# A tuned two-layer matrix kernel: the last third of w1 loaded as float32 by SyncE's queue and cast on chip, x's second half loaded after four strips of w1, five sums of x on GpSimd

## The chip, the cores and the metric

The kernel runs on one core of a Trainium2 chip. The metric is the device time of one execution in microseconds. Before the change three runs gave 852.94, 865.14 and 854.82 us, a median of 854.82 us. The engines are called as in the profile: PE is TensorE (matmuls), PEld its weight loads, DVE VectorE, ACT ScalarE, POOL GpSimd, SP SyncE, which computes nothing and issues transfers. A "q" behind an engine's name is the part of it that issues and waits.

## The reference

x has 16 x 512 = 8192 rows of 768 numbers, w1 is 768 x 3072, w2 is 3072 x 768, all float32.

```python
y = np.matmul(x, w1) + b1
y = np.maximum(y, 0)
return np.matmul(y, w2).astype(np.float32)
```

## The kernel before, in words

Both layers run in float16 with float32 sums in PSUM. Each layer is cut into blocks and multiplied with a bilinear scheme that needs 26 block products where the plain way needs 32. The price is sums: for one block of x 19 sums of blocks (`X_SUMS`, `next_x_sums`, L787, the instruction at L799), for one third of w1 18 sums (`W1_SUMS`, `add_w1_sums`, L807, instruction L811), for one third of w2 18 (`add_w2_part`, L854, instruction L876), and sums of the products on the way out of PSUM.

**First layer.** x is worked in 8 blocks of 1024 rows. w1 has 3072 columns, in three thirds (g = 0, 1, 2) of four strips of 256 columns: strips 0 to 3 are g = 0, 4 to 7 are g = 1, 8 to 11 are g = 2. A strip is 768 x 256 numbers, loaded by one transfer (`load_strip`, L693) from GpSimd's queue, which casts to float16 on the way. It fills two slots of the tile `v`. For blocks 1 to 7 each third is 26 products of six matmuls of 256 columns (L1127), whose results leave PSUM by ACT (L1150, L1155) and DVE (L1161, L1164) into `yo`, 12 slots that lie in the tile `z`. From there they are stored to a scratch tensor `yd` in DRAM by SP's or GpSimd's queue (`add_store_y`, L998, issue L1003).

**Block 0** is special, since w1 is still arriving. Its thirds 0 and 1 are computed the plain way, strip by strip (`plain`, L1011, matmuls L1022, out through ACT at L1036): a unit is one half of a strip's columns times one half of the block's rows, six matmuls of 512 columns or twelve of 256. Third 2 uses the 26 products. The first half of the block's rows (x tiles 0 to 3) comes as float32 over SP's and ACT's queues, the second half (tiles 4 to 7) as two casting transfers over GpSimd's queue (`load_x`, L710, issue L712). Both are transposed on PE (L948). `first_block` (L1058) writes the order of block 0 by hand: EARLY strips with the first half of the rows, the transposes of the second half, these strips with the second half, then the other strips of thirds 0 and 1 with both.

**Blocks 1 to 7** get x row by row: a casting load of 128 rows by GpSimd's queue (`add_load_x`, L765), then a transposing transfer by SP's queue (`add_turn`, L770, issue L774), which must follow the load; `add_rows` is both. Then come the 19 sums.

**Second layer.** 16 half blocks, each 26 products of six matmuls of 384 columns (L1322), with y read back from `yd` by SP's queue and summed by DVE (L1280).

**What sets the order.** The program is a list of tasks with their reads and writes. `Graph.run` (L375) is a planner: it lays the tasks of each engine in an order by assumed durations and assumed landing times (`presets`, L740, holds those of the prologue's loads), and `emit` writes the instructions out in that order. On the chip each engine works through its list strictly in order, and each transfer takes one of eight semaphores of its queue in turn, so an engine that issues a transfer first waits until the transfer eight before it on that queue has landed. `plan` (L1464) says what is put among the products of which block: for block b the loads and transposes of block b + 1 stand in `later` and are added in `between` (L1207). A constant such as `W2_POOL` lists which sums of w2 GpSimd does instead of DVE.

Of the kernel before, what the change touches and what calls it, by code (L numbers as in the profile page):

```python
# [18 lines left out]
P = 128  # L19
# [559 lines left out]
EARLY, AHEAD = 5, 8  # L579

POOL_X = ()
# [6 lines left out]
W2_POOL = ((0, 11), (0, 13), (0, 18), (0, 23), (0, 25), (1, 13), (1, 25))  # L588
# [5 lines left out]
X1_LATE = 2.0  # L594
# [13 lines left out]
class Fast:  # L608
# [93 lines left out]

    def add_stage_w2(self, g, q, h):
        h0 = (6 * q + 2 * g + h) * P
        self.g.add("POOL", 850, lambda: self.nc.gpsimd.dma_start(
            out=self.w2dram[:, g, q:q + 5:4, h * self.NH:(h + 1) * self.NH],
            in_=self.w2[h0:h0 + P, :].rearrange("p (a n) -> p a n", a=2)), lat=15.0, dma=1.4,
            writes=[("w2d", g, q, h)], after=[self.g.last_pe])
# [11 lines left out]
    def prologue(self):  # L720
        nc = self.nc
        for s in range(4):
            (nc.sync, nc.scalar)[s % 2].dma_start(out=self.rows(s),
                                                  in_=self.xf[s * P:(s + 1) * P, :])
            if s == 1:
                self.load_bias()
        self.constants()
        self.load_strip(0, 0, 2)
        self.load_strip(0, 1, 2)
        for strip in range(2, EARLY):  # L730
            self.load_strip(*divmod(strip, 4))
        for s in (4, 6):
            self.load_x(0, s, NZ - 8 + s, 2)
        for strip in range(EARLY, 12):
            self.load_strip(*divmod(strip, 4))
        for _ in range(9):
            nc.tensor.matmul(self.ps[:, 7, 0:P], lhsT=self.ones, rhs=self.ones, start=True,
                             stop=True)

    def presets(self):  # L740
        g = self.g
        at = (9.5, 11.5, 13.5, 15.5, 19.3, 27.6, 30.6, 32.5, 35.8, 39.1, 41.9, 44.8)
        for t in range(12):
            for k in range(2):
                g.preset(("v", t // 4, 2 * (t % 4) + k), at[t] - (0 if t > 1 or k else 1.0))
        for s in range(4):
            for h in range(2):
                g.preset(("z", NZ - 4 + s, h), 21.9 if s < 2 else 24.6)
# [38 lines left out]
    def next_x_sums(self, b, limit=99):  # L787

        slot = self.xs[b]
        while self.todo and self.free and limit:  # L790
# [5 lines left out]
            e = "POOL" if n in POOL_X else "DVE"  # L796
# [5 lines left out]
            self.g.add(e, 552 if e == "DVE" else 2000, add, port=True,  # L802
# [51 lines left out]
    def add_w2_part(self, g):  # L854
# [15 lines left out]
        for groups in FUSE_V2[g]:  # L870
            for o, i, j, sign in left:
# [7 lines left out]
                self.g.add(e, 2400 if e == "POOL" else 151 + 400 * len(groups), add, port=True,  # L879
# [178 lines left out]
    def first_block(self):  # L1058
# [20 lines left out]
        for strip in range(2):  # L1079
# [3 lines left out]
            run(*pair)  # L1083
        early = [plain(strip, j, 0, 2 if strip == 2 else 1)
# [7 lines left out]
        for p in late[1:]:  # L1092
            next(p)
        run(*late, plain(1, 1, 1, 2),
            *(plain(strip, j, 1, 2 if strip == 2 else 1)
              for strip in range(2, EARLY) for j in range(2)))
        self.xs[0] = self.raw_slots(0)
        self.rowed1 = 8 * (self.rowed + list(self.scratch.values()))
        rest = [(strip, m, j) for strip in range(EARLY, 4 * PLAIN) for m in range(2)
                for j in range(2)]  # L1100
        loads = list(range(8 if PLAIN > 1 else 0))
        for strip, m, j in rest:
            if loads:
                self.add_rows(1, loads.pop(0))
            run(plain(strip, j, m))
        for s in loads:
            self.add_rows(1, s)
# [356 lines left out]
    def plan(self):  # L1464
# [10 lines left out]
        for b in range(NB):  # L1475
# [4 lines left out]
            elif b + 1 < NB:  # L1480
                assert not self.todo
                pre = PRE if b > 1 else 0
# [5 lines left out]
                if b + 2 < NB and b:  # L1488
                    self.later += [(2, PRE_AT + PRE_GAP * s, self.add_load_x, (b + 2, s))
                                   for s in range(PRE)]  # L1490
                for n in range(STAGES if b else 0):
                    if staged:
                        self.later.append((*divmod(STAGE_AT + (78 - STAGE_AT) * n // STAGES, 26),
                                           self.add_stage_w2, staged.pop(0)))
            for n in range(EARLY_RATE if b > 2 else 0):
# [94 lines left out]
```

## Time and profile before

| what | before |
|---|---|
| median of 3 runs | 854.82 us (852.94 to 865.14) |
| the profiled execution | 857.22 us, of which 855.6 us is the span from the first to the last instruction |
| PE busy | 837.6 us, 98% of the span |
| DVE, ACT, POOL busy | 701.8, 558.6, 237.7 us |
| granted TensorE clock | 0.999 |
| queue of SP (q1), share of 16 DMA engines | 120.26 MB, 47.0% |
| queue of POOL (q0), share of 16 DMA engines | 71.00 MB, 43.8% |

The page divides the span by engine, by slices of time and by groups of instructions. A row of a group has the line, the engine, the operation, what it writes from what, how many of them, then busy time, mean duration in ns, and the idle time of the engine just before them with what ended it. A row of the timeline has start, duration, engine, line and operation, and in brackets the idle time before it with the releaser. A row of the table by windows has start and end, the length, then for each engine the busy time and the number of instructions, the granted clock, the busy share of the DMA engines (above 1 where packets of several queues overlap) and GB/s. MB counts what is written, so a casting load reads twice that.

### The profile page before, as it was taken

The page shows a single profiled execution, that of the slowest core. Times are in us where ns is not written, and L with a number is a line of the kernel's source. Part 1 is how long each engine was busy: PE and PEld are TensorE (multiplying, and loading weights), DVE is VectorE, ACT ScalarE, POOL GpSimd, SP SyncE. Part 2 cuts the span into 40 slices and gives each one's busy share as a digit, 9 for nine tenths or more (in the row PEclk, how much of TensorE's full clock was granted, in tenths as well). Part 3 has the DMA queues.
Part 4 walks back from the last instruction along what each step waited for, and adds up shares of the span by engine and source line. Part 5 has one row for each costly group of instructions (what it writes and reads, how often), then busy time and mean ns, then how long its engine had stood idle before and what let it go on. Part 6 is the DMA issues. An engine that isn't in the chain of part 4 may idle for free. (4 is left out here: it accounts for less than half of the span.)

```text
span 855.6 us, 17854 instructions
## 1 busy us (share of the span) xinstructions
PE 837.6 (98%) x6263; PEld 612.6 (72%) x6263; DVE 701.8 (82%) x1341; ACT 558.6 (65%) x1252; POOL 237.7 (28%) x400
## 2 busy tenths in 40 slices
PE   8999989999999999999999999999999999999998
PEld 7658878888888888888875666566666665565664
DVE  6869779797988989889899988888777788777773
ACT  4557767878787878787873455565645567757421
POOL 6104455544645446442402201011100011101000
PEclk9999999999999999999999999999999999999999
DMA  9997999999999999998888989978889989988622
GB/s 218 228 229 166 173 229 229 209 217 228 221 216 225 217 221 234 221 282 271 264 254 202 263 271 281 258 207 230 230 244 277 267 209 222 253 219 274 227 74 75
DMA packets 169168, 193.32 MB, mean 226 GB/s; under 512 B 58556, under 2 KB 144644, under 8 KB 169076
## 3 DMA queue, kind: packets, MB, share of 16 engines
q1 hardware_dynamic: 113632, 120.26, 47.0%
q0 software_dynamic: 54976, 71.00, 43.8%
q8 instruction: 49, 0.80, 0.4%
q10 hardware_dynamic: 468, 0.90, 0.3%
q14 instruction: 43, 0.35, 0.1%
HBM read 140.39 MB, written 83.95 MB: 262 GB/s over the span
## 5 line engine op out<-in xcount | busy, mean ns | idle before, releaser
L1322 PE MATMUL ps<-v,z 128*128 128x384 f16 x2496 | 407.1, 326 | 1.7 <-DVE ps L1343 1.0
L1127 PE MATMUL ps<-z,v 128*128 128x256 f16 x3432 | 379.9, 273 | 8.1 <-DVE z L1161 3.1
L1127 PEld LDWEIGHTS <-v 128*128 128x128 f16 x3432 | 335.0, 98 | 53.3 <-issue 10.8
L1322 PEld LDWEIGHTS <-z 128*128 128x128 f16 x2496 | 244.0, 98 | 164.0 <-issue 1.8
L1280 DVE TENSOR_TENSOR z<-z 128x768 f16<-128x768 f16 x448 | 232.7, 553 | 41.7 <-PE ps L1322 23.5
L1003 POOL DMA_DIRECT2D yd<-z x228 | 123.6, 545 | 173.6 <-ACT z L1150 72.1
L1161 DVE CUSTOM_DVE_ANT_0 z<-ps,s 128x512 f16<-128x512 f32 x220 | 143.8, 684 | 25.8 <-PE ps L1127 21.4
L1155 ACT ACTIVATE s<-ps,bt 128x256 f32<-128x256 f32 x352 | 146.6, 478 | 16.2 <-PE ps L1127 10.6
L1339 ACT ACTIVATE s<-ps 128x384 f32<-128x384 f32 (+1 forms) x151 | 73.6, 488 | 121.4 <-PE ps L1322 114.4
L1164 DVE TENSOR_TENSOR s<-ps,s 128x512 f32<-128x512 f32 x132 | 88.8, 683 | 4.6 <-PE ps L1127 3.3
L799 DVE TENSOR_TENSOR z<-z 128x768 f16<-128x768 f16 x152 | 78.2, 551 | 7.5 <-PE ps L1127 6.7
L908 ACT ACTIVATE junk<-z 128x768 f16<-128x768 f16 x94 | 78.8, 838 | 0.9
L1339 ACT ACTIVATE ps<-ps 128x384 f32<-128x384 f32 x80 | 38.0, 475 | 62.5 <-PE ps L1322 59.6
L904 POOL DMA_DIRECT2D z<-in_x_dram x32 | 23.3, 751 | 193.3 <-ACT junk L908 188.1
L1343 DVE TENSOR_TENSOR s<-ps,s 128x384 f32<-128x384 f32 x107 | 59.3, 554 | 13.2 <-PE ps L1322 12.9
L1155 ACT ACTIVATE z<-ps,bt 128x256 f16<-128x256 f32 x132 | 55.3, 497 | 9.8 <-DVE s L1164 9.8
L1164 DVE TENSOR_TENSOR ps<-ps,s 128x512 f32<-128x512 f32 x66 | 45.2, 697 | 16.6 <-ACT s L1155 13.2
L1155 ACT ACTIVATE ps<-ps,bt 128x256 f32<-128x256 f32 x88 | 39.5, 448 | 25.5 <-PE ps L1127 20.6
L1150 ACT ACTIVATE s<-ps 128x512 f32<-128x512 f32 x66 | 39.7, 602 | 21.5 <-DVE z L1161 14.8
L1343 DVE TENSOR_TENSOR s<-s,ps 128x384 f32<-128x384 f32 x62 | 34.2, 552 | 21.1 <-PE ps L1322 20.7
L1022 PE MATMUL ps<-z,v 128*128 128x256 f16 (+1 forms) x264 | 42.7, 321 | 1.3 <-ACT z L1036 1.1
L1150 ACT ACTIVATE z<-ps 128x512 f16<-128x512 f32 x66 | 38.0, 595 | 4.9 <-PE ps L1127 3.7
(58 smaller groups left out, 306.6 us busy)
## 6 DMA issues: line engine op xcount, KB each, us to landing
z<-yd SPq DMA_DIRECT2D x128, 384.0 KB, 6.8
yd<-z POOLq DMA_DIRECT2D x228, 128.0 KB, 3.9
out_dram<-s SPq DMA_DIRECT2D x127, 192.0 KB, 6.3
yd<-z SPq DMA_DIRECT2D x140, 128.0 KB, 3.5
z<-in_x_dram POOLq DMA_DIRECT2D x34, 384.0 KB, 7.6
z<-in_x_dram POOLq DMA_DIRECT2D x56, 192.0 KB, 6.2
v<-w2d SPq DMA_DIRECT2D x36, 192.0 KB, 4.0
w2d<-in_w_dram POOLq DMA_DIRECT2D x24, 192.0 KB, 5.8
```

The costliest lines, as they stand in the source:

```text
L799: (self.nc.gpsimd if e == "POOL" else self.nc.vector).tensor_tensor(out=self.z[:, a], in0=self.z[:, c], in1=self.z[:, d], op=ALU.add if si ...
L908: self.nc.scalar.activation(out=self.junk, in_=src, func=ACTF.Square, accum_out=None if at is None else self.stat[:, at:at + 1])
L1003: (self.nc.gpsimd if e == "POOL" else self.nc.sync).dma_start(out=self.ydram[:, b, slot, g].rearrange("p s m -> p (s m)"), in_=src)
L1127: nc.tensor.matmul(pairs(self.ps[:, at, :])[:, :, j], lhsT=self.v[:, g, w, k * self.QM + j * P:k * self.QM + (j + 1) * P], rhs=x.rearrange ...
L1150: nc.scalar.activation(out=out, in_=ps, scale=float(a), func=func if kind == "out" else ACTF.Copy)
L1155: nc.scalar.activation(out=pairs(out)[:, :, j], in_=pairs(ps)[:, :, j], func=func, scale=float(a), bias=self.bt[:, n, g, j:j + 1])
L1161: nc.vector._custom_dve(TENSOR_ADD_SAT, out=out, in0=ps, in1=s, s0=F_MAX, s1=0.0)
L1164: nc.vector.tensor_tensor(out=out, in0=in0, in1=in1, op=ALU.add if a == c else ALU.subtract)
L1280: self.nc.vector.tensor_tensor(out=self.y_view(a), in0=self.y_view(c), in1=self.y_view(d), op=ALU.add if sign > 0 else ALU.subtract)
L1322: nc.tensor.matmul(self.ps[:, bank[ch].at[0], 0:NH], lhsT=self.y_view(ys[SECOND_U[p]])[:, h // 2, h % 2 * P:(h % 2 + 1) * P], rhs=self.v[: ...
L1339: nc.scalar.activation(out=out, in_=ps, func=ACTF.Copy, scale=float(a))
L1343: nc.vector.tensor_tensor(out=out, in0=in0, in1=in1, op=ALU.add if a == c else ALU.subtract)
```

## The change

- Strips 8 to 11 (g = 2) are no longer loaded by GpSimd's casting transfers in the prologue. `add_strip` loads each as float32 by SP's queue into four slots of `v` that are not yet in use, and two casts of 768 columns turn it into float16: strips 8 and 10 on ACT, 9 and 11 on GpSimd.
- EARLY goes from 5 to 4: x's tiles 4 to 7 stand behind four strips in GpSimd's queue, and block 0 works four strips with the first half of the rows.
- The loads and transposes of block 1's x (eight `add_rows`) are added from the second unit after that on (X1_FROM), in a rewritten loop.
- Sums 2, 6, 7, 8 and 16 of block 1's x go to GpSimd (X1_POOL).
- The first three tiles of block 2's x are loaded during third 2 of block 0 (PRE0 = 3), by `add_load_x`, and their transposes follow in block 1. Before, block 2's eight loads were all issued with their transposes in block 1.
- W2_POOL names eight sums of w2 instead of seven, and the planner's assumed durations and landing times change.

How the order of the engines moves, at the three places that the prediction speaks of (`v` is the tile of w1 and its sums, `z` the one of x, its sums and the outputs' slots, `yd` the scratch tensor):

SP, from the start. Before:

```order
L723 DMA z<-in_x_dram 128x768 x2
L1003 DMA yd<-v 128x512 x8
L1003 DMA yd<-z 128x512 x2
L1003 DMA yd<-v 128x512 x8
L1003 DMA yd<-z 128x512 x10
L774 DMA_TRANSPOSE z<-z 128x6x128 x2
```

and with the change:

```order
L747 DMA z<-in_x_dram 128x768 x2
L1027 DMA yd<-v 128x512 x2
L712 DMA v<-in_w_dram 128x6x256 x4
L1027 DMA yd<-v 128x512 x14
L1027 DMA yd<-z 128x512 x2
L798 DMA_TRANSPOSE z<-z 128x6x128
L1027 DMA yd<-z 128x512 x4
L798 DMA_TRANSPOSE z<-z 128x6x128
```

The four strips stand behind the first two stores of outputs, and block 1's transposes begin after the first two stores of third 1 instead of the last of twelve.

POOL, from the first strip on. Before:

```order
L699 DMA v<-in_w_dram 128x3x256 x4
L699 DMA v<-in_w_dram 128x6x256 x3
L712 DMA z<-in_x_dram 128x2x768 x2
L699 DMA v<-in_w_dram 128x6x256 x7
L712 DMA z<-in_x_dram 128x768 x8
L1003 DMA yd<-z 128x512 x9
L712 DMA z<-in_x_dram 128x768
```

and with the change:

```order
L700 DMA v<-in_w_dram 128x3x256 x4
L700 DMA v<-in_w_dram 128x6x256 x2
L736 DMA z<-in_x_dram 128x2x768 x2
L700 DMA v<-in_w_dram 128x6x256 x4
L722 CAST v<-v 128x768 x2
L736 DMA z<-in_x_dram 128x768
L722 CAST v<-v 128x768 x2
L736 DMA z<-in_x_dram 128x768 x7
L1027 DMA yd<-z 128x512
L823 TENSOR_TENSOR z<-z 128x768
L1027 DMA yd<-z 128x512
L736 DMA z<-in_x_dram 128x768
```

One strip less stands ahead of x's two transfers (128x2x768) and three less behind them. The casts stand among block 1's eight loads of 128x768, and the first load of block 2's x comes after two stores and one sum of x instead of nine stores.

ACT, around the transposes of x's second half (COPY). Before:

```order
L1036 ACTIVATE v<-ps,b1y 128x2x2x128 x8
L1036 ACTIVATE z<-ps,b1y 128x4x128
L954 COPY z<-ps 128x3x128 x2
L1036 ACTIVATE z<-ps,b1y 128x4x128
L954 COPY z<-ps 128x3x128 x2
L1036 ACTIVATE v<-ps,b1y 128x2x2x128 x8
L1036 ACTIVATE z<-ps,b1y 128x4x128 x14
```

and with the change:

```order
L1060 ACTIVATE v<-ps,b1y 128x2x2x128 x7
L978 COPY z<-ps 128x3x128 x2
L1060 ACTIVATE v<-ps,b1y 128x2x2x128
L978 COPY z<-ps 128x3x128 x2
L720 CAST v<-v 128x768 x2
L1060 ACTIVATE v<-ps,b1y 128x2x2x128 x3
L720 CAST v<-v 128x768
L1060 ACTIVATE v<-ps,b1y 128x2x2x128
L720 CAST v<-v 128x768
L1060 ACTIVATE v<-ps,b1y 128x2x2x128 x4
L1060 ACTIVATE z<-ps,b1y 128x4x128 x16
```

The second half of the rows comes two outputs earlier, and four casts stand among the outputs that follow.

The diff, without lines of context:

```diff
@@ -576,22 +576,23 @@
-EARLY, AHEAD = 5, 8
-POOL_X = ()
+EARLY, AHEAD = 4, 8
+CASTS = ("ACT", "POOL", "ACT", "POOL")
+X1_POOL = (2, 6, 7, 8, 16)
-W2_POOL = ((0, 11), (0, 13), (0, 18), (0, 23), (0, 25), (1, 13), (1, 25))
+W2_POOL = ((0, 11), (0, 12), (0, 21), (0, 24), (1, 12), (1, 13), (1, 25), (2, 18))
-X1_LATE = 2.0
+X1_FROM, X1_LATE, PRE0, PRE0_AT = 1, 0.0, 3, 12
@@ -700,6 +701,29 @@
+    def add_strip(self, g, h):
+        at = 8 + 4 * h
+        def rows():
+            return self.v[:, g, at:at + 4].rearrange("p a m -> p (a m)").bitcast(FP32)
+        h0 = (6 * h + 2 * g) * P
+        keys = [("v", g, at + n) for n in range(4)]
+        self.g.add("SP", 600, lambda: self.nc.sync.dma_start(
+            out=rows().rearrange("p (k h) -> p k h", k=6), in_=self.w1.rearrange("(k p) h -> p k h", p=P)[:, :, h0:h0 + 2 * P]),
+            lat=4.0, dma=2.6, writes=keys, after=[self.g.last_pe], spare=1.0)
+        e = CASTS[h]
+        for k in range(2):
+            def cast(k=k):
+                out, src = self.v[:, g, 2 * h + k], rows()[:, 768 * k:768 * (k + 1)]
+                if e == "ACT":
+                    self.nc.scalar.copy(out=out, in_=src)
+                else:
+                    (self.nc.gpsimd if e == "POOL" else self.nc.vector).tensor_copy(out=out,
+                                                                                  in_=src)
+            self.g.add(e, {"ACT": 850, "POOL": 1500, "DVE": 900}[e], cast, reads=keys, port=e != "ACT",
+                       writes=[("v", g, 2 * h + k)])
@@ -731,7 +755,7 @@
-        for strip in range(EARLY, 12):
+        for strip in range(EARLY, 8):
@@ -739,13 +763,13 @@
-        at = (9.5, 11.5, 13.5, 15.5, 19.3, 27.6, 30.6, 32.5, 35.8, 39.1, 41.9, 44.8)
-        for t in range(12):
+        at = (9.5, 11.5, 13.5, 15.5, 23.7, 26.6, 29.5, 32.4)
+        for t in range(8):
-                g.preset(("z", NZ - 4 + s, h), 21.9 if s < 2 else 24.6)
+                g.preset(("z", NZ - 4 + s, h), 18.4 if s < 2 else 20.8)
@@ -793,13 +817,13 @@
-            e = "POOL" if n in POOL_X else "DVE"
+            e = "POOL" if b == 1 and n in X1_POOL else "DVE"
-            self.g.add(e, 552 if e == "DVE" else 2000, add, port=True,
+            self.g.add(e, 552 if e == "DVE" else 1750, add, port=True,
@@ -876,7 +900,7 @@
-                self.g.add(e, 2400 if e == "POOL" else 151 + 400 * len(groups), add, port=True,
+                self.g.add(e, 1750 if e == "POOL" else 151 + 400 * len(groups), add, port=True,
@@ -1081,6 +1105,8 @@
+        for h in range(4):
+            self.add_strip(2, h)
@@ -1091,20 +1117,16 @@
-        run(*late, plain(1, 1, 1, 2),
-            *(plain(strip, j, 1, 2 if strip == 2 else 1)
-              for strip in range(2, EARLY) for j in range(2)))
+        run(*late, plain(1, 1, 1, 2))
-        rest = [(strip, m, j) for strip in range(EARLY, 4 * PLAIN) for m in range(2)
-                for j in range(2)]
-        loads = list(range(8 if PLAIN > 1 else 0))
-        for strip, m, j in rest:
-            if loads:
-                self.add_rows(1, loads.pop(0))
-            run(plain(strip, j, m))
-        for s in loads:
-            self.add_rows(1, s)
+        units = [(strip, 1, j) for strip in range(2, EARLY) for j in range(2)]
+        units += [(strip, m, j) for strip in range(EARLY, 4 * PLAIN) for m in range(2)
+                  for j in range(2)]
+        for n, (strip, m, j) in enumerate(units):
+            if X1_FROM <= n < X1_FROM + 8:
+                self.add_rows(1, n - X1_FROM)
+            run(plain(strip, j, m, 2 if strip == 2 and m else 1))
@@ -1479,19 +1501,19 @@
-                pre = PRE if b > 1 else 0
+                pre = (0, PRE0)[b] if b < 2 else PRE
-                if b + 2 < NB and b:
-                    self.later += [(2, PRE_AT + PRE_GAP * s, self.add_load_x, (b + 2, s))
-                                   for s in range(PRE)]
+            if b + 2 < NB:
+                self.later += [(2, (PRE_AT if b else PRE0_AT) + PRE_GAP * s, self.add_load_x, (b + 2, s))
+                               for s in range(PRE if b else PRE0)]
```

## The prediction

> **What bounds the kernel now.** I read the engine totals first, then the table by windows, cut at the stages (prologue, block 0's plain thirds, its third 2, block 1, blocks 2 to 5, the change to the second layer, the second layer, the end).
>
> ```profile
> PE 837.6 (98%) x6263; PEld 612.6 (72%) x6263; DVE 701.8 (82%) x1341; ACT 558.6 (65%) x1252; POOL 237.7 (28%) x400
> 0.00:8.70 8.70, 6.74 (x43) 6.38 (x44) 1.84 (x4) 2.64 (x4) 7.78 (x23) 1.00 0.85 223
> 8.70:55.50 46.80, 44.02 (x291) 26.96 (x289) 40.38 (x99) 23.22 (x38) 10.81 (x17) 1.00 1.30 226
> 55.50:72.50 17.00, 16.89 (x154) 14.98 (x154) 11.37 (x20) 12.88 (x32) 3.67 (x7) 1.00 0.79 173
> 72.50:122.00 49.50, 44.73 (x400) 38.61 (x398) 38.20 (x67) 36.34 (x86) 26.19 (x49) 1.00 1.14 196
> 122.00:345.00 223.00, 221.92 (x2014) 196.42 (x2013) 198.66 (x343) 179.29 (x427) 113.86 (x206) 1.00 0.99 222
> 345.00:452.00 107.00, 103.57 (x916) 89.06 (x914) 96.69 (x171) 83.93 (x195) 34.10 (x47) 1.00 0.92 261
> 452.00:851.80 399.80, 399.75 (x2458) 240.16 (x2456) 314.27 (x641) 220.00 (x473) 41.24 (x54) 1.00 0.82 226
> 851.80:855.60 3.80, 0.02 (x1) 0.00 (x0) 0.36 (x1) 0.33 (x1) 0.00 (x0) 0.86 0.36 122
> ```
>
> PE bounds it: 837.6 of 855.6 us busy at full clock. Length minus PE's busy time gives the idle time by stage: 2.0, 2.8, 0.1, 4.8, 1.1, 3.4, 0.1 and 3.8 us, 18.0 in all. The change removes no matmul, so it can only act on these 18.0 us or add to them. It edits the first 122 us (2.8 + 4.8 us idle after the prologue) and a few sums before 452. The timeline of PE shows where these 7.6 us lie:
>
> ```profile
> 19.55 1.47 PE L1022 MATMUL ps<-z,v 128*128 128x512 f16 x6 [0.18 <-DMA v<-in_w_dram]
> 22.14 0.84 PE L948 MATMUL ps<-ident,z 128*128 128x128 f16 x12 [1.12 <-DMA z<-in_x_dram]
> 24.83 0.84 PE L948 MATMUL ps<-ident,z 128*128 128x128 f16 x12
> 46.91 8.21 PE L1022 MATMUL ps<-z,v 128*128 128x512 f16 x36 [1.08 <-ACT z L1036]
> 55.54 19.39 PE L1127 MATMUL ps<-z,v 128*128 128x256 f16 x174 [0.42 <-ACT z L1036]
> 85.43 22.83 PE L1127 MATMUL ps<-z,v 128*128 128x256 f16 x204 [0.98 <-ACT z L1155]
> 109.17 1.47 PE L1127 MATMUL ps<-z,v 128*128 128x256 f16 x12 [0.91 <-DVE z L1161]
> 111.12 8.28 PE L1127 MATMUL ps<-z,v 128*128 128x256 f16 x72 [0.48 <-DVE z L1161]
> 121.47 38.70 PE L1127 MATMUL ps<-z,v 128*128 128x256 f16 x346 [2.07 <-DVE ps L1164]
> ```
>
> **x's second half after four strips.** The timeline of POOL shows when loads land, since each issue waits for the load eight before it: strip 3 at 15.9, strip 4 at 19.8, x's first pair of tiles at 22.4, the second pair at 25.1. ACT's outputs of plain units come 1.30 us apart (0.69 + 0.61).
>
> ```profile
> 15.88 0.82 POOL L699 DMA_DIRECT2D v<-in_w_dram  x1 [1.16 <-DMA v<-in_w_dram]
> 19.79 0.82 POOL L699 DMA_DIRECT2D v<-in_w_dram  x1 [3.09 <-DMA v<-in_w_dram]
> 22.38 0.82 POOL L699 DMA_DIRECT2D v<-in_w_dram  x1 [1.77 <-DMA z<-in_x_dram]
> 25.07 0.56 POOL L712 DMA_DIRECT2D z<-in_x_dram  x1 [1.86 <-DMA z<-in_x_dram]
> 34.21 0.69 ACT L1036 ACTIVATE v<-ps,b1y 128x512 f16<-128x512 f32 x1 [0.61 <-PE ps L1022]
> q0 software_dynamic: 3981, 2.44, 119.4%
> q1 hardware_dynamic: 594, 0.54, 14.6%
> ```
>
> PE was ready for x's first pair at 22.14 - 1.12 = 21.0. With one strip's two units gone from ahead of it, it is ready 2 x 1.30 earlier, at 18.4. The pair now follows strip 3 and took 2.6 us when strip 4 was ahead of it: 15.9 + 2.6 = 18.5, a wait of 0.1. That holds if GpSimd's queue keeps its pace. The two queue rows (8 to 22 us) say that it had nearly all of the engines then: it wrote 2.44 MB, so read 4.88, against 0.54 MB on SP's queue, a tenth. Now SP's queue holds four strips of 0.79 MB from about 13 us on. If it takes half, the gap stretches by 0.9/0.5 to 4.7 us (wait 2.2); if a third to a quarter, to about 3.6 (wait 1.1). The second pair is needed 0.84 + 1.30 + 0.65 = 2.8 us after the first lands and comes 2.7, 3.8 or 4.9 us after it: waits of 0, 1.0, 2.1. The sum is 0.1, 2.1 or 4.3 us against 0.18 + 1.12 = 1.3 before, so -1.2, +0.8 or +3.0. I take **+0.8**: SP had little to send before and four transfers in a row now, which is nearer to sharing than to the old tenth, but its strips start later than x's pairs are queued.
>
> A rule speaks for the bad end. The Trainium skill, "DMA: Bandwidth & Descriptors", section "Issuing engines are not separate DMA queues", says that transfers of all engines run on the same 16 DMA engines and interleave, and its "Queues, rings and completion order" that these take turns packet by packet. By that the term would be +3.0. The trace agrees that the engines were full (share 1.30 above); it has no two full queues side by side to show the turns. Its result is the first rival below.
>
> **The rest of block 0.** The waits at 46.91 and 55.54 (1.08 + 0.42) are on ACT, which waited for a free output slot:
>
> ```profile
> 46.17 1.27 ACT L1036 ACTIVATE z<-ps,b1y 128x512 f16<-128x512 f32 x2 [2.21 <-DMA yd<-z]
> L867 ACT ACTIVATE v<-v 128x768 f16<-128x768 f16 x6 | 5.1, 843 | 0.6 <-DMA v<-w2d 0.6
> L672 POOL CAST ident<-ident 128x128 f16<-128x128 f32 x1 | 0.3, 291 | 0.1
> 36.67 16.33 DVE L811 TENSOR_TENSOR v<-v 128x768 f16<-128x768 f16 x32 [1.07 <-DMA yd<-v]
> 57.81 0.69 DVE L1161 CUSTOM_DVE_ANT_0 z<-ps,s 128x512 f16<-128x512 f32 x1 [4.81 <-PE ps L1127]
> ```
>
> Third 1's outputs now start with all slots free, after third 0's, which have staging of their own. But transposes stand among their stores. Between no relief and all of it (0 to -1.5) I take **-1.0**, nearer to all, because three output pairs leave before a slot is needed again. ACT gets four casts; nearest is L867 at 843 ns, so 3.4 us, in 0.61 us gaps of which each unit leaves one. PSUM's eight banks hide a lag of that size; without them it would cost up to 3.4. A cast on POOL is bounded by six of L672's 291 ns, 1.75 us; four make 7.0, beside the 46.8 - 10.8 = 36 us in which POOL was idle in this stage. DVE's sums of third 2 now wait for POOL's last cast: four strips at 3.6 to 4.7 us from about 15 on land the last at 29 to 34, two casts more make 33 to 38. Behind that wait stand some 35 sums of w1. The last 32 ran from 36.67 to 53.0 before, so they may end 2 or 3 us later, and DVE's idle 4.81 us at 57.81 covers that. Counted at nothing. The block: **-0.2**.
>
> **Block 1.** PE's four waits there (0.98, 0.91, 0.48, 2.07) stand behind DVE:
>
> ```profile
> L799 DVE TENSOR_TENSOR z<-z 128x768 f16<-128x768 f16 x152 | 78.2, 551 | 7.5 <-PE ps L1127 6.7 <-ACT z L954 0.4
> 117.52 1.03 DVE L799 TENSOR_TENSOR z<-z 128x768 f16<-128x768 f16 x2 [3.62 <-PE ps L1127]
> 103.22 6.71 SPq L774 DMA_TRANSPOSE z<-z  x2
> L876 POOL TENSOR_TENSOR v<-v 128x768 f16<-128x768 f16 x7 | 11.8, 1699 | 20.5 <-DVE v L876 8.2 <-ACT v L867 6.2 <-PE ps L1127 6.0
> 58.80 0.55 POOL L1003 DMA_DIRECT2D yd<-z  x1 [12.71 <-DVE z L1161]
> 66.91 0.54 POOL L1003 DMA_DIRECT2D yd<-z  x1 [4.96 <-ACT z L1150]
> ```
>
> At 117.52 DVE had stood 3.62 us before sums of block 2's x, whose last transposes left SP only at 103 to 110; the outputs queued behind came late and PE lost 2.07. Now three of these tiles are loaded in block 0's third 2, where the DMA engines had room (share 0.79). The wait of 0.98 falls while DVE does block 1's sums between outputs; five of 19 leave it (5 x 0.55 = 2.8 us) for 5 x 1.70 = 8.5 us on POOL, which sat idle 12.71 and 4.96 us there. Its stores and the loads of block 2 queue behind sums that wait for transposes, which those gaps cover. The 0.91 and 0.48 hang on output slots, which the change doesn't touch. Of 0.98 + 2.07 = 3.05 I take four fifths, **-2.4**; the bounds are all 4.8 removed and, with POOL holding DVE up as below, +5.4.
>
> The eighth w2 sum on POOL saves DVE 0.55 us where PE idles 3.4 us in 107; the new order there may move single waits of up to 1 us either way. **0**.
>
> **The sum** is -0.2 - 2.4 = -2.6 on the profiled execution's 857.2 us (855.6 of span and 1.6 around it): 854.6. The runs' median is 2.4 us below that execution, so 854.8 - 2.6 = **852.2 us**.
>
> **The rivals.** *SP's strips starve x* (slower): at half share the second pair lands at 15.9 + 4.7 + 4.9 = 25.5. It decides from 25.1 on, where the pair landed before, since PE now needs it earlier. Block 1's x is behind the same queue, so block 1 gains nothing: 854.8 + 3.0 = **857.8**. For it: 1.30 of DMA share; against: SP's strips follow two stores and start late.
>
> *POOL blocks DVE* (slower): a sum on POOL and one on DVE exclude each other.
>
> ```profile
> 412.17 1.89 POOL L876 TENSOR_TENSOR v<-v 128x768 f16<-128x768 f16 x1 [4.19 <-DVE v L876]
> 412.01 0.55 DVE L1280 TENSOR_TENSOR z<-z 128x768 f16<-128x768 f16 x1
> ```
>
> The POOL sum that began inside a DVE sum took 1.89 us, not the median of 1.64. If DVE's sums wait likewise, five times 1.64 minus the 2.8 saved is +5.4 at most, half of it +2.7 likely, as outputs from PSUM stand between the sums: 854.8 - 0.2 + 2.7 = **857.3**. The Trainium skill, "SBUF — State Buffer", section "SBUF: two separate sides", states such an exclusive lock for a DVE operation with two SBUF inputs; the 1.89 agrees.
>
> *The waits only move*: DMA work is the same, the slots as few; **854.8**, within 1. For it: each of the waits is a chain of two or three engines.
>
> *All goes*: x's early end, no waits in block 0, none in block 1: -1.2 - 1.5 - 4.8 = -7.5, **847.3**.
>
> **Chances.** 0.43 for the forecast, 0.22 that waits move, 0.15 for starving, 0.13 for all gone, 0.07 for POOL blocking. The range 847.3 to 858.5 reaches both outer cases and leaves out the worst sums of bounds. The forecast's own range, with half the spread of its two terms, is 850 to 854.5. About 2% is what a measurement of this kernel can tell from no change: 17 us. Faster by that would need PE's busy time to shrink (837.7 against 837.6 busy), so 0.01; slower needs several rivals at once, 0.02; the rest is 0.97.
>
> **What would show it.** Right: the transposes of x's second half start at 19 to 20 and 23 to 24 us; the first L1127 product (now L1149) at 54.5 to 56; idle PE time from there over the next 67 us near 2.5 instead of 4.9; no DVE wait of 3 us before block 2's sums; POOL sums at 1.6 to 1.9 us. Wrong: the second pair after 25.1, casts that make ACT wait for SP's strips, DVE sums longer than 0.56 us or gaps beside POOL's, or a new wait of PE on a transpose of x.

## The result, and the profile after

The changed kernel takes 862.72 us (median of 19 runs, 860.45 to 865.11), the kernel before beside it 856.96 us (19 runs, 852.12 to 865.14). The ratio is 1.0076, 95% interval 1.0056 to 1.0095: 0.8% slower where 0.3% faster was forecast, and outside the predicted range. The profiled execution has a span of 862.0 us against 855.6.

PE's timeline of the changed kernel, the rows that answer to those of before:

```profile
18.54 0.84 PE L972 MATMUL ps<-ident,z 128*128 128x128 f16 x12 [0.67 <-DMA z<-in_x_dram]
31.61 2.75 PE L1046 MATMUL ps<-z,v 128*128 128x512 f16 x12 [1.87 <-ACT v L1060]
38.33 12.21 PE L1046 MATMUL ps<-z,v 128*128 128x512 f16 x48 [3.97 <-ACT v L1060]
54.71 13.01 PE L1046 MATMUL ps<-z,v 128*128 128x512 f16 x48 [4.18 <-ACT z L1060]
67.56 35.31 PE L1149 MATMUL ps<-z,v 128*128 128x256 f16 x318
103.14 37.04 PE L1149 MATMUL ps<-z,v 128*128 128x256 f16 x335 [0.27 <-DVE z L1183]
```

Third 2 starts at 67.56 instead of 55.54: 12.0 us lost before it. From there to the end the kernel takes 862.0 - 67.56 = 794.4 us against 800.1: 5.6 us won. The two together, 6.4 us, are the difference of the spans. The table by windows shows both halves:

```profile
8.70:55.50 46.80, 35.76 (x243) 22.81 (x241) 35.51 (x89) 20.64 (x33) 11.07 (x16) 0.94 1.22 246
40.00:44.00 4.00, 4.00 (x14) 1.54 (x13) 3.38 (x7) 1.37 (x2) 4.00 (x8) 0.66 1.11 257
56.00:60.00 4.00, 4.00 (x11) 1.37 (x10) 3.87 (x8) 0.70 (x2) 0.00 (x0) 0.53 0.72 164
72.50:122.00 49.50, 49.09 (x448) 43.51 (x446) 42.49 (x72) 39.42 (x94) 32.16 (x50) 1.00 0.93 193
```

PE idles 46.80 - 35.76 = 11.04 us in the plain stage (before 2.78), and the granted clock fell to 0.66 and 0.53 in 4 us stretches behind the long waits. The groups of PE price that: the 264 plain matmuls were busy 46.9 us, 42.7 before. So 8.3 us of idle time and 4.2 us of slow matmuls make the 12 us, less what the earlier part won. In block 1 PE idles 0.41 us where it idled 4.77 (0.27 us if the stretch is taken 12.0 us later, as third 2 is).

ACT, SP and POOL in the plain stage, from their timelines in turn:

```profile
29.41 1.56 ACT L720 CAST v<-v 128x768 f16<-128x768 f32 x2 [6.31 <-DMA v<-in_w_dram]
34.39 0.83 ACT L720 CAST v<-v 128x768 f16<-128x768 f32 x1 [1.67 <-DMA v<-in_w_dram]
42.72 0.69 ACT L1060 ACTIVATE z<-ps,b1y 128x512 f16<-128x512 f32 x1 [1.87 <-PE ps L1046]
53.97 1.27 ACT L1060 ACTIVATE z<-ps,b1y 128x512 f16<-128x512 f32 x2 [5.30 <-DMA yd<-z]
```

```profile
13.19 10.56 SPq L712 DMA_DIRECT2D v<-in_w_dram  x4
23.86 19.71 SPq L1027 DMA_DIRECT2D yd<-v  x14
43.67 1.61 SPq L1027 DMA_DIRECT2D yd<-z  x2
45.40 1.46 SPq L798 DMA_TRANSPOSE z<-z  x1
46.96 3.92 SPq L1027 DMA_DIRECT2D yd<-z  x4
```

```profile
38.94 1.60 POOL L722 CAST v<-v 128x768 f16<-128x768 f32 x2 [11.44 <-DMA v<-in_w_dram]
40.48 3.72 POOL L736 DMA_DIRECT2D z<-in_x_dram  x7
```

Two things stand out. ACT waits 6.31 + 1.67 us at its casts for strips, and PE's 1.87 and 3.97 us follow. And the first store of third 1 leaves SP at 43.67 us, behind the strips and fourteen third-0 stores. In the kernel before it left at 38.87, and nine more followed with no transpose between them:

```profile
38.87 12.40 SPq L1003 DMA_DIRECT2D yd<-z  x10
```

With the change ACT gets a slot back only at 53.97, and PE's 4.18 us follow that. The two holds end together: the outputs of this first store were ready at 42.72 + 0.69 = 43.41 us, late behind ACT's casts, and SP was done with the fourteen stores at 23.86 + 19.71 = 43.57. Which of the two sets the time is what the runs below had to tell.

### The profile page after: what moved, and what is told of

It reads as the page before. It is cut to its first block, busy times and chain, and to the rows that moved or that the text cites. A ratio compares the mean times of both kernels' runs of the same rounds, so it can differ in the third digit from the quotient of the medians.

```text
span 862.0 us, 17871 instructions
## 1 busy us (share of the span) xinstructions
PE 840.4 (97%) x6263; PEld 614.3 (71%) x6263; DVE 700.6 (81%) x1335; ACT 560.1 (65%) x1256; POOL 248.3 (29%) x406
## 5 line engine op out<-in xcount | busy, mean ns | idle before, releaser
L1149 PEld LDWEIGHTS <-v 128*128 128x128 f16 x3432 | 335.3, 98 | 47.0 <-issue 6.4
L1027 POOL DMA_DIRECT2D yd<-z x228 | 123.6, 545 | 172.6 <-DVE z L1183 71.4
L1046 PE MATMUL ps<-z,v 128*128 128x256 f16 (+1 forms) x264 | 46.9, 340 | 10.4 <-ACT v L1060 5.8
L1046 PEld LDWEIGHTS <-v 128*128 128x128 f16 x264 | 26.6, 101 | 29.7 <-issue 16.5
```

The source lines that it names most:

```text
L1027: (self.nc.gpsimd if e == "POOL" else self.nc.sync).dma_start(out=self.ydram[:, b, slot, g].rearrange("p s m -> p (s m)"), in_=src)
L1046: nc.tensor.matmul(self.ps[:, ps.at[0], cols], lhsT=self.v[:, g, 2 * h + k2, k * self.QM + j * P:k * self.QM + (j + 1) * P], rhs=rhs, star ...
L1149: nc.tensor.matmul(pairs(self.ps[:, at, :])[:, :, j], lhsT=self.v[:, g, w, k * self.QM + j * P:k * self.QM + (j + 1) * P], rhs=x.rearrange ...
```

## The experiments

Theory A: ACT works in order, its casts hold the outputs back. Theory B: the output slots of third 1 come free too late, because of what stands ahead of their stores on SP. Theory C: the strips' bytes slow every transfer. The ratio is to the kernel before, run on the same chip; its median moved between 854.5 and 858.0 us from chip to chip, so ratios are to be compared. The two columns on third 2 are of one profiled execution each.

| run | third 2 starts (us) | from there to the end (us) | median (us) | ratio, interval |
|---|---|---|---|---|
| before | 55.54 | 800.1 | 856.96 | 1 |
| the change | 67.56 | 794.4 | 862.72 | 1.0076, 1.0056 to 1.0095 |
| 1 ACT's casts on DVE | 68.10 | 793.5 | 863.03 | 1.0096, 1.0063 to 1.0129 |
| 2 strips on GpSimd's queue | 61.35 | 794.1 | 856.68 | 1.0014, 0.9989 to 1.0038 |
| 3 ACT held, kernel before | 59.50 | 805.3 | 862.67 | 1.0074, 1.0037 to 1.0110 |
| 4 block 1's x early, kernel before | 57.39 | 796.2 | 858.58 | 1.0039, 1.0008 to 1.0071 |
| 5 as 2, block 1's x late | 56.13 | 797.1 | 854.85 | 0.9976, 0.9955 to 0.9997 |
| 6 the change, block 1's x late | 63.33 | 794.7 | 860.38 | 1.0038, 1.0017 to 1.0059 |
| 7 as 1, block 1's x late | 65.43 | 795.2 | 862.50 | 1.0067, 1.0030 to 1.0104 |
| 8 as 7, third-0 stores on POOL | 64.85 | 794.9 | 861.16 | 1.0062, 1.0038 to 1.0086 |
| 9 as 8, but two of them on SP | 54.63 | 800.8 | 856.47 | 0.9977, 0.9954 to 0.9999 |
| 10 both edits of block 1 alone | 55.30 | 795.8 | 852.71 | 0.9978, 0.9961 to 0.9996 |
| 11 the sums on POOL alone | 55.44 | 796.7 | 852.85 | 0.9968, 0.9942 to 0.9994 |
| 12 the early loads alone | 54.95 | 796.4 | 852.95 | 0.9961, 0.9938 to 0.9985 |
| 13 as 10, block 1's x earlier | 54.80 | 802.6 | 856.28 | 0.9992, 0.9966 to 1.0018 |

**Run 1: ACT's casts on DVE.**

```diff
-CASTS = ("ACT", "POOL", "ACT", "POOL")
+CASTS = ("DVE", "POOL", "DVE", "POOL")
```

> The changed kernel, with ACT's four casts of w1's last third given to DVE; POOL keeps its four, and the order of SP's and POOL's transfers is as in the changed kernel. Theory A (ACT works strictly in order, waits 6.31 + 1.67 us at its casts for SP's strips, and the evictions of PSUM behind them stop PE): PE's waits of 1.87 and 3.97 us on ACT at 31.6 and 38.3 us go, the matmuls of that stretch keep the full clock (1.8 us), and the time falls from 862.7 to 855 to 857; the 4.18 us before the third block of matmuls may stay. Theory B (the loss is in output slots that SP's late stores free too late): under 2 us better, 861 or more. Theory C (SP's four float32 strips slow every transfer, whoever casts them): no gain, 862 to 863. A gain of 10 us or more, 852 or less, would say that ACT's hold is the cause of the later 4.18 us as well.

Theory A fell: nothing was won. The waits at the casts went, and one wait at the slots took their place, ending at the same moment as before the edit (54.09 against 53.97). The outputs of the first third-1 store were now ready at 35.12 + 0.69 = 35.81 us, and it still left SP only at 43.66: here SP alone held it. Timelines of PE and ACT, and 4 us behind the wait by the windows:

```profile
54.83 13.43 PE L1046 MATMUL ps<-z,v 128*128 128x512 f16 x48 [11.97 <-ACT z L1060]
```

```profile
54.09 1.27 ACT L1060 ACTIVATE z<-ps,b1y 128x512 f16<-128x512 f32 x2 [13.10 <-DMA yd<-z]
```

```profile
56.00:60.00 4.00, 4.00 (x11) 1.47 (x10) 3.93 (x9) 0.69 (x1) 0.00 (x0) 0.50 0.72 164
```

**Run 2: the strips back on GpSimd's casting queue**, the rest of the change kept (and the planner's assumed landing times of these strips as before).

```diff
-        for strip in range(EARLY, 8):
+        for strip in range(EARLY, 12):
-        for h in range(4):
-            self.add_strip(2, h)
```

> The changed kernel with the last third of w1 back on GpSimd's casting queue as half precision, so no float32 strips on SP and no casts on chip; four strips ahead of x's second half, the five sums on POOL and the early loads of block 2's x stay. Theories A, B and C alike put the whole loss on the strips: PE's idle time in block 0's plain thirds returns from 11.0 to about 2.8 us, the granted clock stays at 1.0, block 1 keeps its gain of 4.4 us of idle time: 850 to 852.5. If instead block 1 gained only because block 0 was late and its x had more time to arrive, block 1 loses its gain again and the time is 855 to 857. If the shorter lead of w1 (four strips for five) has a price of its own, the first 25 us show a wait of over 1.3 us and the time is 853 to 855.

All three theories gave at most 852.5, and all missed. The time lies where the expectation put a block 1 that loses its gain, but from third 2 to the end the run takes 794.1 us, so the gain is kept. Without any strip on SP, ACT still got its slot only at 53.47 us. SP's waits (total, times, longest in us), SP's timeline and ACT's show why:

```profile
SPq L798 <- DMA z<-in_x_dram: 7.7, 1, 7.7
```

```profile
36.61 0.80 SPq L1027 DMA_DIRECT2D yd<-z  x2
45.16 1.32 SPq L798 DMA_TRANSPOSE z<-z  x1
```

```profile
53.47 1.27 ACT L1060 ACTIVATE z<-ps,b1y 128x512 f16<-128x512 f32 x2 [6.40 <-DMA yd<-z]
```

The change's X1_FROM put block 1's first transpose behind two third-1 stores. It waits 7.7 us for a load that stands behind w1 on GpSimd's queue, and the next stores stand behind the transpose.

**Run 3: ACT held for 7 us in the kernel before.**

```diff
+        def hold():
+            for _ in range(8):
+                self.nc.scalar.activation(out=self.junk, in_=self.v[:, 0, 0], func=ACTF.Copy, scale=1.0)
+        self.g.add("ACT", 0, hold, reads=[("v", 0, 0)], writes=["junk"], after=[self.g.tasks[-1]], due=-1.0)
```

> The kernel before with eight extra copies of a 128 by 768 tile on ACT (some 6.7 us, their output unused) right behind the copies of the transposes of x's second half; no transfer is added, moved or removed. It prices a hold of ACT by itself. Theory A: PSUM's eight banks fill within 3 to 4 us, PE stops for 3 to 5 us, and the granted clock falls below 1.0 for some 4 us after it: 857.0 + 4 to 7 = 861 to 864, with PE's waits in this stage on ACT. Theory C (the loss came with the transfers, ACT's hold is mostly hidden by the banks and by ACT's idle 0.6 us a unit): 857 to 859. Theory D on the clock (idle time of PE alone lowers it): the clock in the 4 us windows behind the longest idle stretch shows 0.5 to 0.95; if the drop belonged to something in the changed kernel's transfers, it stays at 1.0.

The copies on ACT's timeline, PE's wait behind them, and the stretch after it by the windows:

```profile
26.00 6.99 ACT L1094 ACTIVATE junk<-v 128x768 f16<-128x768 f16 x8
```

```profile
35.93 14.80 PE L1022 MATMUL ps<-z,v 128*128 128x512 f16 x60 [3.17 <-ACT v L1036]
```

```profile
36.00:40.00 4.00, 4.00 (x12) 1.44 (x12) 0.56 (x1) 1.14 (x2) 0.90 (x2) 0.57 1.35 229
```

A hold does cost where nothing hides it: eight copies (6.99 us) made PE wait 3.17 us, the next 4 us ran at a clock of 0.57 with no transfer changed, and third 2 started 4.0 us late. PE waited for less than half of it. The profiled execution was this run's slowest (866.38 us, the others from 856.98). After third 2 has started it loses 5.2 us more, with a PE wait of 3.70 us on DVE at 126.77 and a clock of 0.50 from 127 to 131; why stays open.

**Runs 4, 5 and 6: the order on SP.** Run 4 is the kernel before with the change's loop for block 1's x; 5 is run 2, and 6 the change, with that x late again.

```diff
-X1_LATE = 2.0
+X1_FROM, X1_LATE = 1, 0.0
```

```diff
-X1_FROM, X1_LATE, PRE0, PRE0_AT = 1, 0.0, 3, 12
+X1_FROM, X1_LATE, PRE0, PRE0_AT = 8, 0.0, 3, 12
```

(9 instead of 8 in runs 6 to 9.)

> The kernel before with one edit of the change alone: block 1's x is loaded and transposed from the second unit of third 1 on (X1_FROM = 1, X1_LATE = 0), so SP has two third-1 stores ahead of its first transpose of block 1's x instead of ten, and then two stores between transposes. w1 stays on GpSimd's queue, no float32 strips, no casts. Theory B, as the removal of ACT's casts left it (the first transpose waits on SP for a load that lies behind the last strips of w1, and the stores behind it free third 1's output slots late): SP waits 5 to 8 us at its first transpose, ACT 5 to 7 us for a slot, PE 4 to 6 us, with the granted clock at 0.5 to 0.7 for some 4 us after it: 4 to 7 us more than before, some of it paid back in block 1 (its x is there earlier): 856 to 861 beside 854.5 to 857. Rival (the order on SP is harmless, all of the loss is in the float32 strips): no PE wait over 2 us in block 0, 853 to 857.

> The changed kernel with both suspects undone: w1's last third on GpSimd's casting queue, and block 1's x loaded from the ninth unit on (X1_FROM = 8), so that ten third-1 stores stand on SP ahead of the first transpose, as in the kernel before. Four strips ahead of x's second half, five sums on POOL and the three early tiles of block 2 stay. Theory B: the 6.40 us for which ACT waited for a slot in the run with w1 on GpSimd's queue fall to about 2, PE's 5.28 us to under 1.5, the clock stays at 1.0; x's second half gains about 1 us: 850 to 852.5. Rival (that wait came from w1's or x's transfers themselves, not from SP's order): 855 to 857.

> The changed kernel with block 1's x loaded from the tenth unit on (X1_FROM = 9): ten third-1 stores stand on SP ahead of the first transpose; strips on SP and casts on ACT and POOL stay. Two holds are claimed: ACT's casts (PE waits 1.87 + 3.97 us and some 1.8 us of clock) stay; the first third-1 store still leaves SP only at about 43.7 us, behind the strips, but lands in 6 to 7 us instead of 10 as no burst of seven loads runs beside it, and no transpose stands ahead of the next stores, so PE's 4.18 us fall to 0 to 2: 858 to 861. If SP's strips alone set the time: 862 to 863. If the order on SP was the whole loss: 853 to 856.

PE's timelines, of 4 (with a row of the windows), 5 and 6 in turn:

```profile
54.74 2.75 PE L1022 MATMUL ps<-z,v 128*128 128x512 f16 x12 [3.07 <-ACT z L1036]
```

```profile
56.00:60.00 4.00, 4.00 (x31) 2.92 (x30) 0.34 (x1) 3.09 (x7) 0.00 (x0) 1.00 0.96 192
```

```profile
46.77 8.13 PE L1046 MATMUL ps<-z,v 128*128 128x512 f16 x36 [0.83 <-ACT z L1060]
56.13 17.85 PE L1147 MATMUL ps<-z,v 128*128 128x256 f16 x162 [1.22 <-ACT z L1060]
```

```profile
38.63 13.46 PE L1046 MATMUL ps<-z,v 128*128 128x512 f16 x48 [3.51 <-ACT v L1060]
52.69 10.80 PE L1046 MATMUL ps<-z,v 128*128 128x512 f16 x48 [0.60 <-ACT z L1060]
```

Run 4 shows the wait (SP 6.4 us, PE 1.14 + 3.07 us), but with no drop of the clock: third 2 is 1.85 us late and block 1 pays it back, yet the median is 0.4% up. Its profiled execution (855.11 us) was its fastest, so what its median lost is not in the profile. Run 5's waits went about as expected (PE 0.83 + 1.22 us), and its ratio is 0.0038 under run 2's, 3.2 us; its time, 854.85, lies above the expected 850 to 852.5. In run 6 the 4.18 us fell to 0.60 and the ratio from 1.0076 to 1.0038. Theory B holds, but this order is only some 3 us of the loss: with the strips on SP, third 2 still starts 7.8 us late.

**Run 7: both edits** (run 1's casts, X1_FROM = 9).

> The changed kernel with ACT's casts given to DVE and block 1's x from the tenth unit on: the two edits of the runs before together. What is left of the loss is then the float32 strips on SP's queue, ahead of fourteen third-0 stores. If the stores behind the strips are a hold of their own: the first third-1 store still leaves at about 43.7 us (before: 38.9), ACT waits 7 to 10 us for a slot instead of 13.1, PE 6 to 9 us: 858 to 861. If ACT's casts and the order on SP were all: PE waits under 2 us in block 0, and the time is 851 to 854.

The first third-1 store on SP, and PE's wait:

```profile
42.53 10.99 SPq L1027 DMA_DIRECT2D yd<-z  x8
```

```profile
52.17 13.42 PE L1046 MATMUL ps<-z,v 128*128 128x512 f16 x48 [9.04 <-ACT z L1060]
```

The slot waits came just above the expected ranges (ACT 10.2 us, PE 9.04), the time 1.5 us above. With late transposes, ACT's casts still cost nothing: run 7 is no faster than run 6, and in both PE has 48 plain matmuls left when it goes on, at 52.17 and 52.69 us. In run 6 the first third-1 store left at 44.66 us, when its outputs were ready (43.95 + 0.69); in run 7 they were ready at 35.40 + 0.69 = 36.09, and it left at 42.53. So the stores behind the strips are a hold of their own.

**Runs 8 and 9: the stores away from the strips.** In 8 all third-0 stores go by POOL and all casts to DVE; 9 leaves on SP the two stores ahead of the strips.

```diff
-                self.add_store_y(0, 2 * m + r, h, g, reg, r, None if g else 8 + 8 * m + 4 * r + h)
+                self.add_store_y(0, 2 * m + r, h, g, reg, r, None if g else 8 + 8 * m + 4 * r + h,
+                                 "SP" if g or h == m == 0 else "POOL")
```

(In run 8: `"SP" if g else "POOL"`.)

> The changed kernel with all eight casts on DVE, block 1's x from the tenth unit on, and third 0's sixteen stores issued by POOL, so that on SP the third-1 stores stand right behind the four float32 strips. It asks whether the stores held behind the strips were what was left. If so: the first third-1 store leaves SP at 36 to 39 us instead of 43.7, ACT waits under 3 us for a slot, PE is idle under 3 us in the plain thirds and starts third 2 at 55 to 57 us with the clock at 1.0. Then a third hold may come out: DVE's sums of w1's last third stand behind casts that wait for the last strip (38.9 us), and ended at 62.6 us in the changed kernel against 53.0 before; third 2 would now need them from 55 on: PE waits of 3 to 8 us on DVE between 55 and 65, and 856 to 860. Without that hold: 851 to 854. If the stores still land late because the strips fill the engines: idle over 5 us before third 2, 859 to 863.

> As the run with third 0's stores on POOL, but the two stores that stand ahead of the strips stay on SP, so that the strips start at about 13 us as in the changed kernel and leave x's second half its turn at 18 to 19 us; the other fourteen third-0 stores go out from POOL, all casts are on DVE, block 1's x comes late. If the stores queued behind the strips were the last hold on the output slots: the first third-1 store leaves SP at 34 to 39 us, ACT waits under 3 us in all for slots, PE idles under 4 us in the plain thirds at full clock, and third 2 starts at 54.5 to 57.5 us. Then DVE's sums of w1's last third, behind casts of strips that land until 39 us, end at 59 to 63 us instead of 53.0, and if third 2 needs them PE waits 2 to 7 us on DVE between 55 and 66: 854 to 859; if not, 851 to 853.5. If instead the strips' own bytes hold everything up, the store leaves in time but lands 10 us later: PE idle over 6 us before third 2, 859 to 863.

Run 8 missed, and shows something else: with no store ahead of them the strips went out from 1.92 us on, and PE's timeline has x's second half ten microseconds late:

```profile
22.35 6.98 PE L1046 MATMUL ps<-z,v 128*128 128x256 f16 x30 [3.13 <-DMA v<-in_w_dram]
29.16 0.67 PE L972 MATMUL ps<-ident,z 128*128 128x128 f16 x9
```

In run 9 the strips start at 13.5 us again. The timelines of SP, PE and DVE in turn, and the plain stage by the windows:

```profile
35.94 11.47 SPq L1027 DMA_DIRECT2D yd<-z  x10
```

```profile
54.63 5.40 PE L1150 MATMUL ps<-z,v 128*128 128x256 f16 x48 [1.08 <-ACT z L1060]
63.21 15.58 PE L1150 MATMUL ps<-z,v 128*128 128x256 f16 x126 [3.18 <-DVE z L1184]
```

```profile
49.83 12.72 DVE L835 TENSOR_TENSOR v<-v 128x768 f16<-128x768 f16 x25
```

```profile
8.70:55.50 46.80, 44.85 (x301) 27.98 (x299) 36.87 (x95) 24.05 (x39) 15.29 (x26) 1.00 1.19 250
```

The first store leaves at 35.94, PE idles 1.95 us in the plain stage at full clock, third 2 starts at 54.63. So the float32 strips' bytes do the plain stage no harm by themselves (theory C falls); what stood behind them on SP did. One thing more differs from run 7: POOL's casts went to DVE, fourteen stores stand on POOL instead, and the loads of block 1's x behind them leave from 43.46 us instead of 40.74. The first third-1 store took 7.4 us to land beside these loads in run 7, and 5.7 in run 9, where it landed ahead of them (5.8 before). So some 2 us may belong to the loads, against 6.6 us by which the store leaves earlier; no run moves the loads alone. Then the third hold appears, as expected: DVE's sums of w1's last third run until 62.5 us, third 2 needs DVE earlier, PE waits 3.18 us, and from 65 to 67 us the clock is 0.50. From third 2 to the end run 9 takes 5.0 us more than run 10. It is 0.2% faster than before, no better than run 10, which leaves the loads of w1 and x alone.

**Runs 10 to 13: block 1.** Run 10 is the kernel before with both edits, 11 and 12 have one each; 13 is 10 with block 1's x from the fifth unit on.

```diff
-POOL_X = ()
+X1_POOL = (2, 6, 7, 8, 16)
```

```diff
-X1_LATE = 2.0
+X1_LATE, PRE0, PRE0_AT = 2.0, 3, 12
```

> The kernel before with only two edits of the change: five of block 1's sums of x on POOL, and three tiles of block 2's x loaded in block 0's last third. Block 0's loads of w1 and x stay as before. If the gain after 55 us belongs to these edits: block 1's idle time falls from 4.8 to 0.4 to 2.4 us, the time from 857.0 to 852 to 854.6. If it was a gift of the delay (block 0 late, block 1's x early): 856 to 857.5. If POOL's sums block DVE: 858 or more.

> The kernel before with five of block 1's sums of x on POOL and nothing else. If the prediction's reading holds (the 0.98 us wait falls while DVE does block 1's sums, the 2.07 us stand behind late transposes of block 2's x): PE's idle time between 72.5 and 122 us falls from 4.8 by 1 to 2 us, the wait before block 2's sums stays: 0.5 to 2 us faster. If POOL's sums block DVE: no gain or up to 3 us slower, DVE sums over 0.56 us.

> The kernel before with three tiles of block 2's x loaded in block 0's last third and nothing else. If the 2.07 us wait at 121.5 us stands behind late transposes of block 2's x: it goes, DVE's 3.62 us before its sums go, the 0.98 us wait near 85 us stays: 1.5 to 2.5 us faster. If the loads only take DMA time from block 1's x: no change within 1 us.

> The kernel before with the two edits of block 1 (five sums on POOL, three early tiles of block 2) and block 1's x from the fifth unit on (X1_FROM = 4): six third-1 stores ahead of the first transpose, which then comes to its turn at about 46 us, when its load has landed (45.5). If the first transpose has nothing to wait for, block 0 keeps its waits (1.1 + 0.4 us) or loses under 1 us, and block 1 loses most of the 1.6 us that it still idles with the two edits alone: span 849.5 to 851, time 1.5 to 2 us under that run's at the same median of before. Rival (stores among transposes cost what block 1 gains): the same time within 1 us.

PE's busy time in block 1 in runs 10, 11 and 12, a PE wait each of runs 11 and 12, then DVE and PE of run 13:

```profile
72.50:122.00 49.50, 47.91 (x435) 42.26 (x434) 42.29 (x72) 39.44 (x95) 32.41 (x53) 1.00 1.04 207
```

```profile
72.50:122.00 49.50, 47.66 (x433) 42.00 (x431) 40.72 (x68) 39.21 (x95) 31.17 (x51) 1.00 1.10 205
```

```profile
72.50:122.00 49.50, 48.29 (x438) 42.40 (x437) 42.94 (x75) 40.15 (x96) 26.13 (x48) 1.00 0.99 205
```

```profile
83.93 10.26 PE L1127 MATMUL ps<-z,v 128*128 128x256 f16 x90 [1.09 <-DVE z L799]
84.83 55.43 PE L1127 MATMUL ps<-z,v 128*128 128x256 f16 x499 [0.97 <-ACT z L1155]
```

```profile
73.18 1.15 DVE L799 TENSOR_TENSOR z<-z 128x768 f16<-128x768 f16 x2 [6.46 <-DMA z<-z]
```

```profile
74.99 24.15 PE L1123 MATMUL ps<-z,v 128*128 128x256 f16 x198 [6.27 <-DVE ps L1160]
```

Either edit alone takes the idle time from 4.77 to 1.84 or 1.21 us, both together to 1.59: the gains do not add. In all three the waits after 109 us go (0.91, 0.48 and 2.07 before), and the one near 85 us, 0.98 before, stays: 1.26, 1.09 and 0.97 us. So run 11's 2.07 us wait went, against expectation. That either edit is enough to let DVE keep up is argued, not shown.

Runs 10, 11 and 12 took 852.28 to 854.08, 851.93 to 856.57 and 852.06 to 853.30 us; the kernel before took 851.79 to 860.75 beside run 10 and 851.44 to 861.33 beside the other two. The lowest times are alike: what the edits take away is the upper part of the spread. The profile of before (857.22 us) lies in that part, so its 4.77 us need not stand in every execution.

Run 13 gained nothing, as its rival said: its median is some 3.4 us above runs 11 and 12 on the same chip. In its profile, which is its slowest execution (858.89 us, the others from 851.56), a sum of x waits in DVE's order for a transpose, and PSUM work stands behind it. No run beat 10, 11 and 12, which can't be told from one another.

## Why the prediction was wrong

- **The step that failed** is the rest of block 0. "Third 1's outputs now start with all slots free" was true and not enough: the term had no price for how late the stores that free the slots leave. Fourteen third-0 stores and then third 1's stood on SP behind four strips. SP's waits in the changed kernel have `SPq L1027 <- DMA v<-in_w_dram: 5.5, 2, 4.1`: with eight semaphores in turn, a store cannot be issued before the transfer eight places ahead has landed, and for two stores that was a strip. The predicted -1.0 us became +8.3 us of idle time and 4.2 us of slow matmuls. Run 7, with ACT's casts and the early transposes gone, still starts third 2 at 65.43; run 9, which moves the stores, starts it at 54.63.
- "But transposes stand among their stores" was seen, but only as a reason to take less gain. It costs some 3 us (2 against 5, the change against 6).
- "Four strips at 3.6 to 4.7 us from about 15 on land the last at 29 to 34": SP's strips were cast at 24.9, 29.4, 34.4 and 38.9 us, 4.5 to 5 us apart, and SP stood 10.56 us in issuing the four.
- Casts "counted at nothing" because "PSUM's eight banks hide a lag of that size": the cast's length was priced (0.83 us measured, 0.843 forecast), not the 8.0 us that ACT waits for the data. It was named as a sign of error and still had no term. That it cost nothing more was luck: the slots came free no earlier without it (runs 1 and 7). By run 3 a hold of 7 us, had it been alone, is worth 4 us.
- DVE's w1 sums "may end 2 or 3 us later": they ended at 63.7 us instead of 53.0 (the last two after a wait for PE, the others at 60.0). The late third 2 covered that; run 9 uncovers it, 3.18 us.
- **No term for the clock.** The prediction multiplied idle times by one. The Trainium skill, "TensorE: Matmul & The Clock Gate", section "HAM oscillation — how this bites in real kernels", warns of idle gaps of PE over about 3.4 us, behind which matmuls run at half clock. The traces agree in kind, at a shorter gap: 3.07 us idle left the clock at 1.00 (run 4), 3.17 us brought 0.57 (run 3), 3.18 us brought 0.50 (run 9), 11.97 us brought 0.50 (run 1). So, as far as these single profiles tell, a wait here begins to cost more than its length a little over three microseconds.
- **x's second half** came at the good end: PE waited 0.67 us for the first pair, at 18.54 us, not for the second, and 0.36 us between them for DVE's copies, so that +0.8 was nearer -0.3. The turns packet by packet that the prediction weighs are in the trace. Its two queues from 16 to 19 us, then from 22 to 30:

```profile
q0 software_dynamic: 299, 0.43, 79.8%
q1 hardware_dynamic: 296, 0.27, 33.8%
```

```profile
q1 hardware_dynamic: 1370, 1.37, 62.2%
q0 software_dynamic: 1369, 0.68, 61.9%
```

Both queues moved the same number of packets. But turns are not halves of the time: up to 19 us, with x's pairs on it, GpSimd's queue (q0) had the larger packets and held the engines more than twice as long as SP's; later, with w1's strips, both held them alike. And SP's strips, issued from 13.19 us on, have no packet in the trace before 15 us, when x was nearly there. So the step from turns to half of the engines, and to +3.0 us, failed; turns did not. (A third to a quarter would also stretch 2.6 us to 3.1 to 3.5, not to the 3.6 that the middle case has.) The rival of starved x is real: in run 8, with the strips sent at once, the queues take turns from 8 to 22 us (2399 and 2398 packets, 62.0% and 61.4%), and x is there only at 29.16. Nor did being early win anything: run 5 with x's pair at 18.95 has the same ratio as run 10 with it at 21.80.
- **Block 1** came out near its number, by luck: -2.4 us forecast, 3.2 us of idle time gone in run 10 and 1.8 us of its median. The forecast took the gain from the waits of 0.98 and 2.07 us and left 0.91 and 0.48 alone; in runs 10 to 12 the 0.98 stays and the other three go. That late transposes of block 2's x alone stood behind the 2.07 us is not borne out either: the row of DVE's 3.62 us names PE as the releaser, and run 11 leaves these loads as they were. In the changed kernel all four waits are gone, but there block 1's x also had more time, and the two are not separated. POOL's sums hardly held DVE up: DVE's sums of x took 559 ns in the mean, 551 before.
- **w2** at nothing stands: PE idles 3.68 us from 351.4 to 458.4, against 3.43 from 345 to 452 before.

## What to carry to other kernels

When a transfer is moved to another queue, list everything that is behind it on that queue, to the end of the stage, and follow each to what it frees. The cost of these strips was in small stores whose slots the outputs needed. The largest wait in a profile need not be the bound: two holds that end at the same time hide each other, and taking away one of them wins nothing (run 1). Before a gain is read from one profile, see how far that execution lies above the lowest time of its kernel. And count a new PE wait of over 3 us with the slow matmuls behind it.

## What the runs showed of the hardware

Waits of 3.97 and 4.18 us were followed by stretches at 0.66 and 0.53 of full clock, and 48 matmuls took 12.21 and 13.01 us: 0.254 and 0.271 us each, against 8.21/36 = 0.228 in the row of before at 46.91. SP issued the first two strips of 768 KB in 0.43 and 0.58 us, but the third and fourth held it for 5.14 and 4.27 us. While both had work, the queues of SP and GpSimd moved packet for packet, and the one with the larger packets had more of the engines' time. Casts of 128x768 from float32 to float16 took 0.83 us on ACT, 0.83 to 1.15 on POOL and 0.56 on DVE.
